# Runs of sixteen products, split down-weight loads and a finer end in a two-layer decoder trunk

## The chip, the cores and the metric

The kernel runs on one core of one Trainium2 chip. The core has a matrix engine (TensorE, PE in the profile, with its weight loads shown as PEld), a vector engine (VectorE, DVE), a scalar engine (ScalarE, ACT), GpSimd (POOL) and SyncE (SP), which here only sends DMA transfers. Each engine runs its own instruction list in order, and they wait for one another by semaphores. The metric is the device time in microseconds (us) of one execution. The kernel before takes 2140.93 us, the median of three runs (2140.59 to 2141.5).

## The reference

Two layers over 256 tokens of width 2048, all in float32. Each layer does, cut to what matters here:

```python
h = rmsnorm(x, attn_norm_g[l])
q, k, v, gate_b, gate_c, conv_in = split(h @ w_in[l])        # six parts of 1024 columns
attn = rmsnorm(diff_attention(rmsnorm(q), rmsnorm(k), v), subln_g[l])
conv = gate_b * short_conv(gate_c * conv_in, conv_w[l])      # causal, 3 taps
x = x + concat([attn, conv]) @ w_out[l]                      # 2048 x 2048
hm = rmsnorm(x, mlp_norm_g[l]) @ w_up[l]                     # 2048 x 8192
x = x + square(relu(hm)) @ w_down[l]                         # 8192 x 2048
```

The weights are read once; they are most of the traffic. The products are most of the work.

## The kernel before

**Numbers in two parts.** Every float32 operand of a product is split into a hi part and a lo part that the matrix engine can multiply, and a product is the sum of three: hi by hi, hi by lo, lo by hi. For weights ACT writes hi (a copy that rounds) and DVE writes lo (the original minus hi); in the program's names `whi` and `wlo`, and for the up projection `uhi` and `ulo`. Activations are kept as both parts side by side, so a matmul with the weight's hi part can take both parts of the activations at once. That is a wide matmul, 128x512; the one with the weight's lo part needs the hi part of the activations alone, and is narrow, 128x256.

**Weights.** `Weights.take()` hands out the next tile (hi, lo) of a list of jobs, and makes the tiles up to three ahead (`AHEAD`): it sends the DMA of a raw tile on SP's queue and puts the conversions on ACT and DVE. There are three buffers each for hi and lo (`wpool`), four for raw tiles. A conversion therefore waits for its raw tile to land and for PE to be done with the tile three before it; a load waits until the lo conversion of the tile four before it has read its buffer.

**Order of the work.** PE's list is exactly the order in which the program writes the matmuls (`manual_schedule`). ACT's, DVE's, SP's and POOL's lists are ordered by a scheduler that places each operation by its estimate of when it is ready and wanted, so that a change on PE moves operations on the others too. Small pieces of work (norms, attention, convolution) are kept as generators in `Background` and put between the matmuls by `work.tick()`.

**The mixer (q, k, v, conv).** `linear` does q, k, v and the output projection. `linear_t` (L392) does the three projections of the convolution branch, gate_C (`gc`), conv_in (`ci`) and gate_B (`gb`), with weights stationary: for each of four columns of 256 it goes through four weight tiles of 512x256, and for each tile through eight wide and then eight narrow matmuls. The gc and ci columns alternate, and beside them the attention of the second half of the heads runs in the background: scores (`sc`), the attention output's norm (`an`), its transposition (`atp`) and its split into `cat`. When the last attention buffers come free, the first four transfers of up weights (`uraw`, 1 MB each) are sent.

**The MLP, up.** 32 pairs of 2 x 128 hidden columns. A column's up projection (`up_part`, L941) takes two weight tiles of 1024 rows, and does eight wide and eight narrow matmuls with each; the result in the single bank tagged `av` (`upc`) is read by ACT as `ev` (L961), added by DVE to `h`, and for a pair squared and split into `f` (`square`, L964 to L984). From pair 2 on each column is followed by products of the pair two before (`LAG`) with rows of the down weights: a Strassen-like scheme that has seven products for eight, products 1, 2, 3 and 5 after the first column and 7, 6 and 4 after the second (`product`, L991). Its weights come from `quarters` (L833): `load_rows` (L826) sends one 1 MB transfer of two K tiles of 128 rows (`draw`), and from it come `b1h`, `b1l` (the first K tile's first half), `b2h`, `b2l` (the second K tile), the sums `t` and their halves `t13h`, `t13l`, `t24h`, `t24l` (L841 to L859). Two buffers hold the raw rows.

**The MLP, down.** The second half of the output columns is accumulated in blocks from the hidden values, which went out to DRAM as `hid`. At the end of a layer `onto` (L1049) adds an accumulator to the residual `xs`. In the last layer the very last block is done `by_token` (L1125): token tile 0 first over all of K, then tile 1. Then both tiles are added and `store` (L1112) sends them as two transfers on SP's queue.

Of the kernel before, what the change touches and what calls it, by code (L numbers as in the profile page):

```python
# [9 lines left out]
F32 = mybir.dt.float32  # L10
# [5 lines left out]
P = 128  # L16
# [3 lines left out]
NT = S // P  # L20
# [8 lines left out]
CH = 512  # L29
WC = 256  # L30
KG = 4
# [74 lines left out]
def trunk(ctx: ExitStack, tc: tile.TileContext, x, w_in, w_out, conv_w, q_norm_g, k_norm_g,  # L106
          lambda_q1, lambda_k1, lambda_q2, lambda_k2, subln_g, attn_norm_g, mlp_norm_g,
          w_up, w_down, rel_bias, selector, out):
    nc = tc.nc
# [8 lines left out]
    mm = ctx.enter_context(tc.tile_pool(name="mm", bufs=2, space=PSUM))  # L118
# [7 lines left out]
    def bank(name):  # L126
        return ps.tile([P, CH], F32, tag="bank", name=name)
# [264 lines left out]
    def linear_t(name, acts, weights):  # L392

        acc = mm.tile([P, 2, 2, S], F32, tag="mm2", name=name)
        nk = len(acts) * KG
        for k0 in range(0, nk, 4):
            hi, lo = weights.take()  # L400
            a = acts[k0 // KG]
            while not a.ready:
                work.tick()
            for part, wt in ((0, hi), (1, lo)):
                for k in range(k0, k0 + 4):
                    for f in range(2):
                        fs = slice(f * P, (f + 1) * P)
                        nc.tensor.matmul(  # L408
                            acc[:, f, 0] if part else acc[:, f], wt[:, k % 4, fs],
                            a.ap[:, 0, k % KG] if part else a.ap[:, :, k % KG],  # L410
                            start=(part == 0 and k == 0), stop=(part == 1 and k == nk - 1),
                            skip_group_check=True)
                    if k % 2:
                        work.tick()
        return acc
# [374 lines left out]
    def mlp(l, mnorm, last):  # L790
# [5 lines left out]
        with ExitStack() as scope:  # L796
# [28 lines left out]

            def load_rows(i, col, pool=dpool, tag="draw"):  # L826
                raw = pool.tile([P, 2, 2 * CH], F32, tag=tag, name=tag)
                nc.sync.dma_start(
                    raw, w_down[l][i * 2 * P:(i + 1) * 2 * P, col:col + 2 * CH].rearrange(
                        "(k p) c -> p k c", p=P))  # L830
                return raw

            def quarters(i, col=0):  # L833
# [104 lines left out]
                acc = ps.tile([P, CH], F32, tag="av", name="upc", bufs=1)  # L938
                return acc.rearrange("p (h s) -> p h s", h=2)

            def up_part(acc, kh):  # L941

                hi, lo = weights.take()
                for part, wt in ((0, hi), (1, lo)):
                    for k in range(8):
                        a = mT[kh * 2 + k // KG]
                        while not a.ready:
                            work.tick()  # L950
                        nc.tensor.matmul(  # L951
                            acc[:, 0] if part else acc, wt[:, k],
                            a.ap[:, 0, k % KG] if part else a.ap[:, :, k % KG],
                            start=(part == 0 and kh == 0 and k == 0),
                            stop=(part == 1 and kh == 1 and k == 7), skip_group_check=True)
                        if k % 4 == 3:
                            work.tick()

            def evict(acc, dst):
                ev = nat.tile([P, 2, S], F32, tag="wide", name="ev")  # L960
# [37 lines left out]
            for i in range(NP):  # L998
                j = i - LAG
                end = i == NP - 1  # L1000
                h = fpool.tile([P, 8, P], F32, tag="h", name="h", bufs=1)
                if i == 0:
                    two = mm.tile([P, 2, CH], F32, tag="mm2", name="up0")
                    two = [two[:, c].rearrange("p (h s) -> p h s", h=2) for c in range(2)]
                    for kh in range(2):
                        for c in range(2):
                            up_part(two[c], kh)
                    forms["plain"]()
                    for c in range(2):
                        evict(two[c], h[:, 2 * c:2 * c + 2])  # L1010
                    fs[0] = square(0, h)
                    forms["sums"]()
                    continue
                for c in range(2):
                    if i < LAG:
                        acc = bank("upw").rearrange("p (h s) -> p h s", h=2)
                    else:
                        acc = column_bank()
                    up_part(acc, 0)
                    up_part(acc, 1)  # L1020
                    evict(acc, h[:, 2 * c:2 * c + 2])
                    if c == 1:
                        fs[i] = square(i, h)
                    if j == 0 and c == 0:
                        for pair in ((1, 6), (2, 3)):
                            w2 = mm.tile([P, 2, CH], F32, tag="mm2", name=f"pr{l}{pair[0]}")
                            prods[pair[0]], prods[pair[1]] = w2[:, 0], w2[:, 1]
                        for n in (4, 5, 7):
                            prods[n] = bank(f"pr{l}{n}")
                    if j >= 0 and c == 0:  # L1030
                        b11, b21, b22 = weights.take()
                        t1, t3 = weights.take()
                        f = fs[j]
# [75 lines left out]
                    pair(2 * b + j, f, 4 * j)  # L1109
                return f  # L1110

            def store(n):  # L1112
                for t in range(NT):
                    nc.sync.dma_start(
                        out[0, t * P:(t + 1) * P, n * CH:(n + 1) * CH], xs[n][:, t])

            if last:
                store(0)
                store(1)


            accs = [mm.tile([P, NT, CH], F32, tag="mm2", name=f"dn{l}{n}") for n in range(2)]
            prods[2], prods[4] = accs[0][:, 0], accs[0][:, 1]
            prods[3], prods[8] = accs[1][:, 0], accs[1][:, 1]

            def by_token(f, n):

                parts = [weights.take() for _ in range(KG // 2)]
                for t in range(NT):
                    for k in range(KG):  # L1130
                        for m, (pa, pw) in enumerate(TERMS):
                            nc.tensor.matmul(
                                accs[n][:, t], f(k, pa, t), parts[k // 2][pw][:, k % 2],
                                start=False, stop=(k == KG - 1 and m == 2))
                        work.tick()

            def columns(f, n, start=False, stop=False):

                for kp in range(KG // 2):
                    hi, lo = weights.take()  # L1140
                    for k in (2 * kp, 2 * kp + 1):
                        for t in range(NT):
                            for m, (pa, pw) in enumerate(TERMS):
                                nc.tensor.matmul(  # L1144
                                    accs[n][:, t], f(k, pa, t), (hi, lo)[pw][:, k % 2],
                                    start=(start and k == 0 and m == 0),
                                    stop=(stop and k == KG - 1 and m == 2))
                        work.tick()
# [4 lines left out]
            for i in range(2 * BLK):  # L1153
# [6 lines left out]
                    continue  # L1160
                start, end = i == SEVEN[0], i == SEVEN[-1]
                if start:
                    for n in (1, 5, 6):
                        prods[n] = bank(f"pr{l}r{n}")
                    prods[7] = ps.tile([P, CH], F32, tag="av", name=f"pr{l}r7", bufs=1)
                b11, b21, b22 = weights.take()
                t1, t3 = weights.take()
# [14 lines left out]
            for b, n in order:  # L1182
                if n == 0 and b + 1 < NB2 - 1:
                    blocks[b + 1] = block(b + 1)
                units = lambda k, pa, t, f=blocks[b]: f[:, pa, 2 * k + t]
                if last and (b, n) == order[-1]:
                    by_token(units, n)
                else:
                    columns(units, n, stop=(b == NB2 - 2))
                if b == NB2 - 2:  # L1190
                    for t in range(NT):
                        onto(xs[2 + n][:, t], accs[n][:, t], xs[2 + n][:, t])
                    if last:
                        store(2 + n)
                    else:
                        work.start(norm.chunk(2 + n, (5, 2)[n]))
        return norm

# [45 lines left out]
```

## Time and profile before

| | |
|---|---|
| runs (three) | 2140.59 to 2141.5 us, median 2140.93 |
| profiled execution | 2141.7 us, its span 2139.9 us |
| TensorE clock granted | 1.00 |
| PE | 2129.0 us busy, 99%, 10,925 matmuls |
| DVE | 1699.2 us, 79% |
| ACT | 1316.2 us, 62% |
| chain that ended last | PE 97%, DVE 1%, ACT 1%, DMA 1% |
| largest groups of the chain | upc (L951) 31%, pr (L994) 13%, dn (L1076) 8%, o (L386) 8% |
| DMA | 476 MB, 222 GB/s over the span; 277 GB/s between 420 and 440 us |
| DVE between 420 and 440 us, and between 700 and 780 | 19.86 of 20, 70.56 of 80 |

The profile is of one execution. A row of a timeline has the start in us, the length, the engine, the line of the kernel, the operation, its result and operands, the shapes and a count where equal operations are joined; in square brackets stands the time in which the engine was idle before it and what ended that. A row of waits has the time in all, how many times and the longest. An "SPq" row is the sending of a DMA, not its transfer. The length of a matmul contains its filling and draining, which overlap with its neighbours, so that the time of a run of matmuls is read from start to start.

### The profile page before, as it was taken

What the parts mean: (1) busy time and instruction counts of PE and PEld (TensorE: products, weight loads), DVE (VectorE), ACT (ScalarE), POOL (GpSimd) and SP (SyncE); (2) the same over time, 40 slices, a digit from 0 to 9 for tenths busy, and PEclk for the clock granted to TensorE, in tenths of its full rate; (3) what the DMA queues carried; (4) which work ended last, traced back from release to release, by engine and by line L of the source; (5) the groups of instructions that cost most, each with busy time, mean ns of one, the idle gap of its engine ahead of it and who ended that gap; (6) DMA issues with size and microseconds to landing.
All of it is one profiled execution on the core that took longest, in us unless ns stands there. A gap on an engine that the chain in (4) does not pass through costs nothing.

```text
span 2139.9 us, 28980 instructions
## 1 busy us (share of the span) xinstructions
PE 2129.0 (99%) x10925; PEld 1817.0 (85%) x10925; DVE 1699.2 (79%) x2315; ACT 1316.2 (62%) x1776; POOL 164.3 (8%) x226
## 2 busy tenths in 40 slices
PE   9999999999999999999999999999999999999999
PEld 8888888888888888888888888888888888888887
DVE  6778655798888888798666776557888888888986
ACT  6666545666666666566566664446666666665653
POOL 3110200000000000001101101000000000000110
PEclk9999999999999999999999999999999999999999
DMA  7555866677777777788656558656777777777983
GB/s 273 178 162 168 257 187 187 195 243 229 234 233 229 229 236 225 240 301 302 219 177 178 167 162 262 188 167 213 240 235 221 241 228 226 237 226 258 317 307 121
DMA packets 296221, 475.98 MB, mean 222 GB/s; under 512 B 10804, under 2 KB 191622, under 8 KB 296081
## 3 DMA queue, kind: packets, MB, share of 16 engines
q1 hardware_dynamic: 267232, 406.88, 60.9%
q0 software_dynamic: 28800, 67.24, 9.4%
q8 instruction: 85, 1.39, 0.3%
q14 instruction: 56, 0.45, 0.1%
q10 hardware_dynamic: 48, 0.02, 0.0%
HBM read 440.52 MB, written 33.58 MB: 222 GB/s over the span
## 4 chain that ended last, share of the span: by engine, by line
PE 97%; DVE 1%; ACT 1%; DMA 1%; issue 0%; DVEq 0%; ACTq 0%
PE upc L951 31%; PE pr L994 13%; PE dn L1076 8%; PE o L386 8%; PE ci L408 4%; PE gb L408 4%; PE q L386 4%; PE k L386 4%; PE v L386 4%; PE gc L408 4%; PE dn L994 2%; PE dn L1144 2%; PE pr1r L994 1%; PE pr0r L994 1%; PE upw L951 1%; PE up L951 1%
## 5 line engine op out<-in xcount | busy, mean ns | idle before, releaser
L303 DVE TENSOR_TENSOR wlo<-raw,whi 128x1024 fp32r<-128x1024 f32 x274 | 341.7, 1248 | 221.1 <-ACT whi L302 219.6
L302 ACT ACTIVATE whi<-raw 128x1024 fp32r<-128x1024 f32 x274 | 290.4, 1060 | 306.8 <-PE o L386 73.6
L951 PE MATMUL upc<-nT,uhi 128*128 128x512 f32 x1920 | 477.6, 391 | 0.8 <-ACT ev L961 0.8
L818 ACT ACTIVATE uhi<-uraw 128x1024 fp32r<-128x1024 f32 x256 | 271.3, 1061 | 279.4 <-PE upc L951 259.8
L951 PEld LDWEIGHTS upc<-nT,uhi 128*128 128x128 f32 x1920 | 352.7, 188 | 69.4 <-ACT ev L961 1.2
L819 DVE TENSOR_TENSOR ulo<-uraw,uhi 128x1024 fp32r<-128x1024 f32 x256 | 312.5, 1221 | 108.8 <-ACT uhi L818 104.9
L951 PEld LDWEIGHTS upc<-nT,ulo 128*128 128x128 f32 x1920 | 261.9, 190 | 18.7
L951 PE MATMUL upc<-nT,ulo 128*128 128x256 f32 x1920 | 267.7, 282 | 0.0
L1076 PE MATMUL dn<-whi,fb 128*128 128x512 f32 x528 | 166.1, 389 | 0.0
L386 PE MATMUL o<-whi,cat 128*128 128x512 f32 x512 | 159.5, 390 | 0.0
L302 ACT ACTIVATE whi<-uraw 128x1024 fp32r<-128x1024 f32 x66 | 70.0, 1061 | 84.0 <-PE dn L1076 79.0
L1076 PEld LDWEIGHTS dn<-whi,fb 128*128 128x128 f32 x528 | 99.1, 188 | 20.6
L386 PEld LDWEIGHTS o<-whi,cat 128*128 128x128 f32 x512 | 96.1, 188 | 19.7
L842 DVE TENSOR_TENSOR t13l<-t,t13h 128x1024 fp32r<-128x1024 f32 x81 | 99.1, 1224 | 5.4 <-ACT t13h L841 3.3
L1076 PE MATMUL dn<-wlo,fb 128*128 128x512 f32 x264 | 102.7, 389 | 0.0
L841 ACT ACTIVATE b2h<-draw 128x1024 fp32r<-128x1024 f32 x81 | 85.6, 1057 | 25.3 <-PE pr L994 22.1
L842 DVE TENSOR_TENSOR b2l<-draw,b2h 128x1024 fp32r<-128x1024 f32 x81 | 98.7, 1218 | 2.3 <-ACT b2h L841 2.3
L842 DVE TENSOR_TENSOR t24l<-t,t24h 128x1024 fp32r<-128x1024 f32 x81 | 98.7, 1219 | 1.5 <-ACT t24h L841 0.3
L386 PE MATMUL o<-wlo,cat 128*128 128x512 f32 x256 | 99.6, 389 | 0.0
L855 DVE TENSOR_TENSOR t<-draw 128x1024 f32<-128x1024 f32 x81 | 98.7, 1218 | 0.5
L303 DVE TENSOR_TENSOR wlo<-uraw,whi 128x1024 fp32r<-128x1024 f32 x66 | 80.5, 1222 | 19.7 <-ACT whi L302 19.5
L994 PE MATMUL pr<-t13h,f 128*128 128x512 f32 x240 | 93.8, 391 | 0.0
(408 smaller groups left out, 4109.7 us busy)
## 6 DMA issues: line engine op xcount, KB each, us to landing
uraw<-in_w_up_dram SPq DMA_DIRECT2D x128, 1024.0 KB, 6.6
raw<-in_w_in_dram SPq DMA_DIRECT2D x191, 512.0 KB, 3.9
draw<-in_w_down_dram SPq DMA_DIRECT2D x85, 1024.0 KB, 5.5
uraw<-in_w_down_dram SPq DMA_DIRECT2D x33, 1024.0 KB, 5.8
raw<-in_w_out_dram SPq DMA_DIRECT2D x64, 512.0 KB, 3.7
hid0p<-f POOLq DMA_DIRECT2D x20, 512.0 KB, 6.9
raw<-in_w_down_dram SPq DMA_DIRECT2D x10, 1024.0 KB, 5.1
fb<-hid0p POOLq DMA_DIRECT2D x20, 512.0 KB, 6.9
```

The lines of the kernel that those rows point to most:

```text
L302: pair = (nc.scalar.activation(hi, raw, AF.Copy), nc.vector.tensor_sub(lo, raw, hi.bitcast(F32)))
L303: nc.vector.tensor_sub(lo, raw, hi.bitcast(F32)))
L386: nc.tensor.matmul(acc[:, t], a.ap[:, pa, k % KG, t * P:(t + 1) * P], (hi, lo)[pw][:, j], start=(k == 0 and n == 0), stop=(k == nk - 1 and ...
L408: nc.tensor.matmul(acc[:, f, 0] if part else acc[:, f], wt[:, k % 4, fs], a.ap[:, 0, k % KG] if part else a.ap[:, :, k % KG], start=(part ...
L818: pair = (nc.scalar.activation(hi, src, AF.Copy), nc.vector.tensor_sub(lo, src, hi.bitcast(F32)))
L819: nc.vector.tensor_sub(lo, src, hi.bitcast(F32)))
L841: keep(nc.scalar.activation(hi, src, AF.Copy))
L842: keep(nc.vector.tensor_sub(lo, src, hi.bitcast(F32)))
L855: keep(nc.vector.tensor_sub(t[:, 0:2], raw[:, :, 1], raw[:, 0]))
L951: nc.tensor.matmul(acc[:, 0] if part else acc, wt[:, k], a.ap[:, 0, k % KG] if part else a.ap[:, :, k % KG], start=(part == 0 and kh == 0 ...
L994: nc.tensor.matmul(prods[n], f[:, pa, a], b[pw], start=(start and m == 0), stop=(stop and m == 2))
L1076: nc.tensor.matmul(prods[p], f[:, pa, 2 * k + t], b[pw][:, n], start=(p in starts and k == 0 and m == 0), stop=(stop and k == 1 and m == 2))
```

## The change

- `linear_t` takes two tiles at a time and does sixteen wide matmuls, then sixteen narrow ones.
- `up_part` takes several halves; for pairs 1 to 31 a column's two tiles are done as sixteen wide and sixteen narrow ones. Pair 0 stays in eights.
- `load_rows` sends two transfers of 512 KB, one for each K tile.
- The banks of products 4, 5 and 7 are allocated in the order 5, 7, 4; in the last layer the second pair of accumulators of the down blocks are two single banks, and products 1 and 5 of the second stage share one two-bank tile.
- `store` sends one token tile, right after that tile is added; the last tile of the last block is added and sent in two halves of 256 columns, the first on SP's queue, the second on ACT's.

All matmuls, conversions and bytes are the same as before.

```diff
@@ linear_t
-        for k0 in range(0, nk, 4):
-            hi, lo = weights.take()
-            a = acts[k0 // KG]
-            while not a.ready:
-                work.tick()
-            for part, wt in ((0, hi), (1, lo)):
-                for k in range(k0, k0 + 4):
+        for k0 in range(0, nk, 8):
+            tiles = [weights.take() for _ in range(2)]
+            for part in range(2):
+                for k in range(k0, k0 + 8):
+                    a = acts[k // KG]
+                    while not a.ready:
+                        work.tick()
+                    wt = tiles[(k - k0) // 4][part]
                     for f in range(2):
...
@@ load_rows
-                nc.sync.dma_start(
-                    raw, w_down[l][i * 2 * P:(i + 1) * 2 * P, col:col + 2 * CH].rearrange(
-                        "(k p) c -> p k c", p=P))
+                for k in range(2):
+                    nc.sync.dma_start(
+                        raw[:, k], w_down[l][(i * 2 + k) * P:(i * 2 + k + 1) * P,
+                                             col:col + 2 * CH])
@@ up_part
-            def up_part(acc, kh):
+            def up_part(acc, *halves):
-                hi, lo = weights.take()
-                for part, wt in ((0, hi), (1, lo)):
-                    for k in range(8):
...
+                tiles = [weights.take() for _ in halves]
+                for part in range(2):
+                    for kh, wt in zip(halves, tiles):
+                        for k in range(8):
...
-                    up_part(acc, 0)
-                    up_part(acc, 1)
+                    up_part(acc, 0, 1)
-                        for n in (4, 5, 7):
+                        for n in (5, 7, 4):
                             prods[n] = bank(f"pr{l}{n}")
@@ accumulators of the down blocks
-            accs = [mm.tile([P, NT, CH], F32, tag="mm2", name=f"dn{l}{n}") for n in range(2)]
-            prods[2], prods[4] = accs[0][:, 0], accs[0][:, 1]
-            prods[3], prods[8] = accs[1][:, 0], accs[1][:, 1]
+            def two_banks(name):
+                both = mm.tile([P, NT, CH], F32, tag="mm2", name=name)
+                return [both[:, t] for t in range(NT)]
+            accs = [two_banks(f"dn{l}0"),
+                    [bank(f"dn{l}1{t}") for t in range(NT)] if last else two_banks(f"dn{l}1")]
+            (prods[2], prods[4]), (prods[3], prods[8]) = accs
...
-                    for n in (1, 5, 6):
-                        prods[n] = bank(f"pr{l}r{n}")
+                    prods[1], prods[5] = (two_banks(f"pr{l}r1") if last else
+                                          [bank(f"pr{l}r{n}") for n in (1, 5)])
+                    prods[6] = bank(f"pr{l}r6")
@@ end
-                        onto(xs[2 + n][:, t], accs[n][:, t], xs[2 + n][:, t])
-                    if last:
-                        store(2 + n)
-                    else:
+                        if last and (n, t) == (1, NT - 1):
+                            for half, queue in enumerate((nc.sync, nc.scalar)):
+                                at = slice(half * WC, (half + 1) * WC)
+                                onto(xs[3][:, t, at], accs[n][t][:, at], xs[3][:, t, at])
+                                store(3, t, half, queue)
+                            continue
+                        onto(xs[2 + n][:, t], accs[n][t], xs[2 + n][:, t])
+                        if last:
+                            store(2 + n, t)
+                    if not last:
                         work.start(norm.chunk(2 + n, (5, 2)[n]))
```

More of the change, by code (lines that the diff above doesn't have):

```diff
@@ L939, in column_bank @@
                 return acc.rearrange("p (h s) -> p h s", h=2)
-            def up_part(acc, kh):
-                hi, lo = weights.take()
-                for part, wt in ((0, hi), (1, lo)):
-                    for k in range(8):
[L948 to L957, printed above, removed]
+            def up_part(acc, *halves):
[3 more added lines that the diff above has]
+                        for k in range(8):
+                            a = mT[kh * 2 + k // KG]
+                            while not a.ready:
+                                work.tick()
+                            nc.tensor.matmul(
+                                acc[:, 0] if part else acc, wt[part][:, k],
+                                a.ap[:, 0, k % KG] if part else a.ap[:, :, k % KG],
+                                start=(part == 0 and kh == 0 and k == 0),
+                                stop=(part == 1 and kh == 1 and k == 7), skip_group_check=True)
+                            if k % 4 == 3:
+                                work.tick()
             def evict(acc, dst):
@@ L1110, in block, with store @@
                 return f
[L1112 to L1115, printed above, removed]
+            def store(n, t, half=None, queue=nc.sync):
+                at = slice(0, CH) if half is None else slice(half * WC, (half + 1) * WC)
+                queue.dma_start(
+                    out[0, t * P:(t + 1) * P, n * CH + at.start:n * CH + at.stop], xs[n][:, t, at])
             if last:
-                store(0)
-                store(1)
-            accs = [mm.tile([P, NT, CH], F32, tag="mm2", name=f"dn{l}{n}") for n in range(2)]
-            prods[2], prods[4] = accs[0][:, 0], accs[0][:, 1]
-            prods[3], prods[8] = accs[1][:, 0], accs[1][:, 1]
+                for n in range(2):
+                    for t in range(NT):
+                        store(n, t)
+            def two_banks(name):
[4 more added lines that the diff above has]
+            (prods[2], prods[4]), (prods[3], prods[8]) = accs
             def by_token(f, n):
@@ L1132, in by_token @@
                             nc.tensor.matmul(
-                                accs[n][:, t], f(k, pa, t), parts[k // 2][pw][:, k % 2],
+                                accs[n][t], f(k, pa, t), parts[k // 2][pw][:, k % 2],
                                 start=False, stop=(k == KG - 1 and m == 2))
@@ L1144, in columns @@
                                 nc.tensor.matmul(
-                                    accs[n][:, t], f(k, pa, t), (hi, lo)[pw][:, k % 2],
+                                    accs[n][t], f(k, pa, t), (hi, lo)[pw][:, k % 2],
                                     start=(start and k == 0 and m == 0),
```

## The prediction

> **What bounds the kernel now.** I read the page's busy times first, then the waits of TensorE (PE), and only then the timelines at those places.
>
> ```profile
> PE 2129.0 (99%) x10925; PEld 1817.0 (85%) x10925; DVE 1699.2 (79%) x2315; ACT 1316.2 (62%) x1776; POOL 164.3 (8%) x226
> ...
> L951 PE MATMUL upc<-nT,uhi 128*128 128x512 f32 x1920 | 477.6, 391 | 0.8 <-ACT ev L961 0.8
> ```
>
> ```profile
> PE pr L994 <- DVE f L984: 3.2, 2, 1.7
> PE sc L604 <- DVE cat L682: 1.2, 2, 0.6
> PE upc L951 <- ACT ev L961: 0.8, 1, 0.8
> ```
>
> PE is busy for 99% of the span, so the time is that of its matmuls, in an order written by hand. Only three things can move it: what one matmul takes, the few microseconds in which PE waits (these rows: in total, times, longest), and what lies behind its last matmul. The change keeps every matmul; it alters the order of widths, who is late at the waits, and the end. The sum is made against the profiled execution, 2141.7 us (span 2139.9 and 1.8 around it), which stands 0.8 above the median of 2140.93.
>
> **Runs of one width.** A column of the up projection and its neighbours:
>
> ```profile
> 702.04 1.98 PE L951 MATMUL upc<-nT,uhi 128*128 128x512 f32 x8
> 703.85 1.12 PE L951 MATMUL upc<-nT,ulo 128*128 128x256 f32 x8
> 704.80 2.00 PE L951 MATMUL upc<-nT,uhi 128*128 128x512 f32 x8
> 706.64 1.11 PE L951 MATMUL upc<-nT,ulo 128*128 128x256 f32 x8
> ```
>
> From start to start, eight wide matmuls take 1.81 us behind products as wide as themselves and 1.84 behind a narrow run. So a change from narrow to wide costs 0.03, less some 0.01 that the narrow run may get back and that rounding hides: I take 0.02, with ends 0.01 and 0.03. With sixteen and sixteen one such change goes in each of 124 up columns (31 pairs, 2 columns, 2 layers; pair 0 stays) and two in each of 24 columns of linear_t (three projections, 4 columns, 2 layers): 172 x 0.02 = **-3.4 us**, ends -1.7 and -5.2. A sentence apart: the Trainium skill ("TensorE: Matmul & The Clock Gate", Back-to-back issue gap) gives the spacing as a function of the moving width alone, by which the order of widths is worth nothing and the sum below would be 3.4 us higher; the 0.03 between 1.81 and 1.84 speaks against it, and it is a rival below.
>
> **What sixteen in a row needs earlier.** In linear_t the second tile's hi half is now wanted straight behind the first, one narrow run (0.95) earlier, and the lo buffer of the first tile is freed 1.8 us later. Each pair of tiles also sends two loads. With three buffers of each half a tile is elsewhere converted well ahead of its use; not where the norm's release sends the first up weights (four transfers of 1 MB) among the loads of the last ci column:
>
> ```profile
> 231.16 0.37 SPq L343 DMA_DIRECT2D raw<-in_w_in_dram  x1
> 232.60 3.17 SPq L811 DMA_DIRECT2D uraw<-in_w_up_dram  x3
> 235.87 4.55 SPq L343 DMA_DIRECT2D raw<-in_w_in_dram  x1
> ```
>
> ```profile
> 247.27 1.06 ACT L302 ACTIVATE whi<-raw 128x1024 fp32r<-128x1024 f32 x1 [2.00 <-DMA raw<-in_w_in_dram]
> 251.34 1.06 ACT L302 ACTIVATE whi<-raw 128x1024 fp32r<-128x1024 f32 x1 [3.01 <-DMA raw<-in_w_in_dram]
> ```
>
> ```profile
> 244.37 2.00 PE L408 MATMUL ci<-nT,whi 128*128 128x512 f32 x8
> 246.21 1.11 PE L408 MATMUL ci<-nT,wlo 128*128 128x256 f32 x8
> 247.16 2.00 PE L408 MATMUL ci<-nT,whi 128*128 128x512 f32 x8
> ```
>
> Before, the second ci tile was issued at 231.16, ahead of the up weights; the third came behind three of them (235.87) and could be converted only at 247.27, the fourth at 251.34. In the changed program's SP queue it is the second tile that stands behind three up weights (its issue waits for a lo conversion that now comes after the norm's an), and the third behind all four. Transfers of one queue land in turn, so the second tile gets the place of the row at 247.27: hi ready at 248.33, wanted at 244.37 + 1.81 = 246.2, late by 2.1. The third gets 251.34, ready at 252.40, wanted 3.7 after the second began, at 252.05: late by 0.35 more. The squares in front of the norm no longer queue behind a whi of 1.06 on ACT, so I let the up weights go some 0.7 earlier: 1.4 + 0.35 + 0.1 for PE's restart = 1.9. Layer 1:
>
> ```profile
> 1310.44 1.06 ACT L302 ACTIVATE whi<-raw 128x1024 fp32r<-128x1024 f32 x1 [2.53 <-DMA raw<-in_w_in_dram]
> ```
>
> ```profile
> 1307.02 2.00 PE L408 MATMUL ci<-nT,whi 128*128 128x512 f32 x8
> ...
> 1315.56 2.11 PE L408 MATMUL ci<-nT,whi 128*128 128x512 f32 x8
> ```
>
> Likewise 1311.50 against 1308.8, less 0.7, with 0.45 behind it, is 2.4; some 0.3 of waiting at 1315.56 is in the time already. Together **+4.0 us**, ends +1.0 (up weights 2 us earlier) and +5.4 (no earlier).
>
> Scores wait for cat (1.2 us in the second rows above):
>
> ```profile
> 163.17 0.74 DVE L682 SCALAR_TENSOR_TENSOR cat<-atp,s_gain,cat 128x512 fp32r<-128x512 f32 x1
> 163.83 1.21 DVE L303 TENSOR_TENSOR wlo<-raw,whi 128x1024 fp32r<-128x1024 f32 x1
> ```
>
> The lo conversion that stood behind cat now stands ahead of it, on a DVE that must wait for the freed lo buffer first; cat ends some 0.3 later in each layer: **+0.6**, ends -1.2 (the wait vanishes) and +2.4 (the whole 1.2 in both).
>
> **Start of the MLP.** The long waits for f go back to late down weights:
>
> ```profile
> 445.71 0.37 SPq L811 DMA_DIRECT2D uraw<-in_w_up_dram  x1
> 446.31 0.40 SPq L828 DMA_DIRECT2D draw<-in_w_down_dram  x1
> ```
>
> ```profile
> 456.44 0.63 ACT L841 ACTIVATE b1h<-draw 128x512 fp32r<-128x512 f32 x1 [4.21 <-DMA draw<-in_w_down_dram]
> ...
> 1520.61 0.63 ACT L841 ACTIVATE b1h<-draw 128x512 fp32r<-128x512 f32 x1 [5.47 <-DMA draw<-in_w_down_dram]
> ```
>
> That draw was issued right behind an uraw and held ACT for 4.21 and 5.47 us, and with it the squares and f. In the changed order it goes ahead of that uraw, in two halves, so b1h needs only the first. The waits for f and ev, 3.2 + 0.8 and about 0.8 for restarts and rounding, go: **-4.8**. What is late next, with the first down rows of the product phase:
>
> ```profile
> 417.96 1.22 DVE L819 TENSOR_TENSOR ulo<-uraw,uhi 128x1024 fp32r<-128x1024 f32 x1
> 419.10 1.22 DVE L842 TENSOR_TENSOR t13l<-t,t13h 128x1024 fp32r<-128x1024 f32 x1
> ```
>
> ```profile
> 428.68 0.63 ACT L841 ACTIVATE b1h<-draw 128x512 fp32r<-128x512 f32 x1 [0.58 <-DMA draw<-in_w_down_dram]
> 429.22 1.05 ACT L841 ACTIVATE b2h<-draw 128x1024 fp32r<-128x1024 f32 x1
> ```
>
> ```profile
> 421.29 0.39 PE L994 MATMUL pr<-t13l,f 128*128 128x512 f32 x1
> ...
> 429.37 1.98 PE L951 MATMUL upc<-nT,uhi 128*128 128x512 f32 x8
> ```
>
> A second ulo now stands ahead of t13l: 419.10 + 1.14 + 1.22 = 421.5 against 421.3, 0.2 late. And b1h, an uhi and b2h stand ahead of the eviction ev (0.6) that frees the single column bank for the column at 429.37; before, ev came first. The second half lands about when the whole did (428.68): b2h ends at 429.7, ev at 430.2, 0.6 late after the 0.2. Layer 1:
>
> ```profile
> 1493.41 0.63 ACT L841 ACTIVATE b1h<-draw 128x512 fp32r<-128x512 f32 x1 [2.40 <-DMA draw<-in_w_down_dram]
> ```
>
> ```profile
> 1492.28 1.98 PE L951 MATMUL upc<-nT,uhi 128*128 128x512 f32 x8
> ```
>
> There b2h starts at 1493.4 at best and ev ends at 1495.0 for 1492.28, 2.5 late with the 0.2. New waits 1.0 + 2.7 = **+3.7** with restarts, ends 0 and +6. Net -1.1.
>
> **Other edits.** The added DMA issues (0.37 each on SP, which mostly waits) delay the uraw behind them by as much; uraws are converted far behind their landing, so nothing; without that cover 0.4 per pair would reach PE. Products in the order 5, 7, 4 and the other accumulator banks sit behind PE's matmuls: nothing. The end:
>
> ```profile
> 2135.02 0.39 PE L1132 MATMUL dn<-whi,fb 128*128 128x512 f32 x1
> ```
>
> ```profile
> 2135.45 1.41 DVE L1049 SCALAR_TENSOR_TENSOR x<-dn,rowf,x 128x512 f32<-128x512 f32 x2 [4.03 <-PE dn L1132]
> ```
>
> ```profile
> DMA to landing us min/median/max: 2.1/4.6/9.2
> ```
>
> by_token finishes token tile 0 first, but one accumulator over both banks kept DVE waiting 4.03 us for the whole, then two updates took 1.41. With single banks tile 0 is updated under tile 1's matmuls, and tile 1 follows in halves of some 0.4: the last store is sent 2 x 0.70 - 2 x 0.38 = 0.65 earlier and lands in about 2.1 as before. **-0.65**, ends -0.3 (a half costs nearly a whole) and -0.9.
>
> **Sum.** 2141.7 - 3.4 + 4.0 + 0.6 - 1.1 - 0.65 = 2141.15 for a profiled execution, less the 0.8 above: **2140.4 us** in the median. I forecast no change that can be told: about 0.2%, 4.3 us, is what a measurement of this kernel can tell from none (2136.6 to 2145.2).
>
> **Rivals.** *The new waits don't come* (faster). The up weights and the first down halves go out earlier than I read from the order. Without new waits at the MLP's start 3.7 less, 2136.7; with the ci tiles at their early end 3.0 less as well, 2133.7; without any new wait about 2132. For it: sixteen matmuls of cover on either side, and draws that go ahead of the uraws. Against it: in both layers the SP queue put one load in its place behind three transfers, and the rows at 247.27 and 1310.44 show what that place costs.
>
> *The split rows land late* (slower). In the changed order b1h and b2h stand ahead of an eviction in every pair, and there is one column bank.
>
> ```profile
> raw<-in_w_in_dram SPq DMA_DIRECT2D x191, 512.0 KB, 3.9
> draw<-in_w_down_dram SPq DMA_DIRECT2D x85, 1024.0 KB, 5.5
> ```
>
> Landing is 3.9 for a half's size against 5.5 for a whole: two in turn would be 7.8, 2.3 more. It decides once b2h ends behind its column's last matmul in the steady pairs and not in the first alone; at 0.13 us in each of 62 pairs it costs 8: 2148. A sentence apart: the Trainium skill ("DMA: Bandwidth & Descriptors", Measured) asks for transfers of 1 MiB or more, and its fit of 2.0 us plus bytes at 436 GB/s gives halves 3.2 each against 4.4; if they are paid in series that is 2.0 more per row. Against it: the conversions at 251.34 and 252.73 follow two loads of 512 KB only 1.39 apart, so loads in one queue overlap all but their bytes.
>
> ```profile
> 252.73 1.06 ACT L302 ACTIVATE whi<-raw 128x1024 fp32r<-128x1024 f32 x1 [0.33 <-DMA raw<-in_w_in_dram]
> ```
>
> *The runs bring nothing*: 1.84 is what a restart behind a narrow run costs wherever it stands, and the sum is 2143.8.
>
> **Chances.** My forecast 0.40, its own range 2137 to 2144 (its terms each within half of their ends). New waits absent or halved 0.37, from 2132 to 2136.6. Split rows late 0.19, from 2145.2 up. Runs that bring nothing 0.04. So faster 0.37, within 0.2% 0.44, slower 0.19. The range for 8 in 10 reaches to 2133 (a tenth lies below, all waits gone) and to 2147 (a tenth above).
>
> **What would show it.** Right: wide matmuls in the up columns 1.81 per eight throughout; PE waits of 1 to 2.5 us for whi in the last ci column of both layers, for ev early in both MLPs, and none for f; two half updates of some 0.4 behind PE's last matmul in place of 1.41. Wrong: any wait for ev or b1l in the steady product phase; no wait in ci; eight wide ones still 1.84 behind another wide run; waits at places I haven't named, since two loads and two conversions at a time move every small operation of the attention beside linear_t by up to 1.2 us.

## The result, and the profile after

The changed kernel takes 2147.49 us (median of six runs, 2145.76 to 2150.48) against 2141.30 (six runs, 2140.59 to 2141.8): 1.0027 of the time before, with a 95% interval of 1.0017 to 1.0038. It is slower, by 6.2 us, just outside the predicted range and on the side that was given a chance of 0.19. A second measurement beside other kernels gave 1.0028 (1.0018 to 1.0038), with one execution at 2154.1. Its runs also spread more: 4.7 and 9.3 us against 1.2 and 3.6.

The profiled execution took 2146.97 us, its span is 2145.2. The waits of PE in it (in total, times, longest):

```profile
PE sc L605 <- DVE cat L683: 4.8, 2, 2.4
PE ci L409 <- ACT whi L302: 2.6, 2, 1.6
PE upc L954 <- ACT ev L964: 1.9, 2, 1.2
PE warm L160 <- DVE mhalf L152: 1.1, 1, 1.1
PE pr L997 <- DVE t13l L844: 0.8, 2, 0.4
PE q L386 <- DVE wlo L303: 0.3, 1, 0.3
```

The waits for f are gone; the one for cat is four times what it was, and those for ci, ev and t13l come where they were foreseen. The second finding is in the clock. Behind the first wait for cat, PE's timeline reads:

```profile
162.54 1.09 PE L409 MATMUL gc<-nT,whi 128*128 128x512 f32 x4
163.47 0.22 PE L605 MATMUL sc<-kT,qT 128*128 128x128 f32 x1
166.07 0.55 PE L605 MATMUL sc<-kT,qT 128*128 128x256 f32 x1 [2.38 <-DVE cat L683]
166.42 0.63 PE L605 MATMUL sc<-kL,qT 128*128 128x128 f32 x2
166.85 0.63 PE L605 MATMUL sc<-kT,qT 128*128 128x128 f32 x2
167.27 0.63 PE L605 MATMUL sc<-kL,qT 128*128 128x128 f32 x2
167.70 5.13 PE L409 MATMUL gc<-nT,whi 128*128 128x512 f32 x12
172.67 2.08 PE L409 MATMUL gc<-nT,wlo 128*128 128x256 f32 x16
```

and the windows over the same stretch (busy time and count of each engine, then PEclk, the granted TensorE clock, the DMA share and GB/s):

```profile
164.00:166.00 2.00, 0.00 (x0) 0.00 (x0) 2.00 (x4) 0.50 (x1) 0.00 (x0) 0.91 0.84 261
166.00:168.00 2.00, 1.93 (x8) 1.96 (x9) 0.96 (x4) 0.00 (x0) 0.00 (x0) 0.50 0.81 235
168.00:170.00 2.00, 2.00 (x6) 1.52 (x6) 0.99 (x7) 0.30 (x1) 0.00 (x0) 0.50 0.08 28
170.00:172.00 2.00, 2.00 (x7) 1.52 (x6) 0.00 (x0) 2.00 (x8) 0.00 (x0) 0.50 0.00 0
172.00:174.00 2.00, 2.00 (x15) 1.85 (x14) 0.12 (x1) 1.57 (x4) 0.00 (x0) 0.89 0.00 0
174.00:180.00 6.00, 6.00 (x38) 5.35 (x37) 5.51 (x10) 2.73 (x3) 1.30 (x1) 1.00 0.53 161
```

The clock is granted at 0.50 from 165.6, while PE still idles, until 172.5. Twelve wide matmuls take 4.97 us from start to start, 0.41 each against 0.23. PE is "busy" all through it, so the page's 99% shows nothing. The same wait in layer 1 (2.39 us) had no such stretch behind it in this execution.

Putting PE's position in the two programs side by side gives the account of the 5.3 us in the spans. Each term is the change of the distance between the same matmul before and after:

| part | layer 0 | layer 1 | worked out before |
|---|---|---|---|
| start, wait for a wlo at 18 us | +0.3 | | not named |
| scores waiting for cat, and the clock behind it | +4.7 | +1.7 | +0.6 for the two together |
| last ci column | +2.3 | +1.1 | +4.0 for the two together |
| start of the MLP, with gb's runs | +0.1 | -1.7 | -1.1, the runs apart |
| runs: gc and ci, steady up columns | -1.3 | -1.3 | -3.4 in all |
| end | | -0.65 | -0.65 |

The runs: a column of the steady up phase is 708.50 to 714.03, 5.53 us, where the rows of before had 702.04 to 707.60, 5.56. A single pair of rows is too coarse for this. In layer 0 the up column that starts at 471.35 before starts 7.03 us later after the change, and the one 52 columns on, at 885.61, starts 6.00 later: 0.02 us gained in each.

```profile
708.50 3.79 PE L954 MATMUL upc<-nT,uhi 128*128 128x512 f32 x16
712.12 2.08 PE L954 MATMUL upc<-nT,ulo 128*128 128x256 f32 x16
714.03 0.40 PE L997 MATMUL pr<-b1h,f 128*128 128x512 f32 x1
```

**Why cat was late.** The rows of DVE and ACT ahead of the wait at 163.47. After:

```profile
163.38 0.75 DVE L761 SCALAR_TENSOR_TENSOR v<-v,rowf,v 128x512 fp32r<-128x512 f32 x1 [0.43 <-ACT v L760]
164.05 1.21 DVE L303 TENSOR_TENSOR wlo<-raw,whi 128x1024 fp32r<-128x1024 f32 x1
165.18 1.40 DVE L683 SCALAR_TENSOR_TENSOR cat<-atp,s_gain,cat 128x512 fp32r<-128x512 f32 x2
```

```profile
160.63 2.01 ACT L302 ACTIVATE whi<-raw 128x1024 fp32r<-128x1024 f32 x2
162.66 0.69 ACT L760 ACTIVATE v<-v,rowf 128x512 fp32r<-128x512 f32 x1
163.25 1.26 ACT L682 ACTIVATE cat<-atp,s_gain 128x512 fp32r<-128x512 f32 x2
```

and ACT, and v on DVE, before (the prediction shows the cat and the wlo behind it, at 163.17 and 163.83):

```profile
160.27 1.06 ACT L302 ACTIVATE whi<-raw 128x1024 fp32r<-128x1024 f32 x1
161.36 0.69 ACT L759 ACTIVATE v<-v,rowf 128x512 fp32r<-128x512 f32 x1
162.51 0.74 DVE L760 SCALAR_TENSOR_TENSOR v<-v,rowf,v 128x512 fp32r<-128x512 f32 x1
```

Two whi in a row stand ahead of v's evacuation on ACT, v's on DVE waits for that, and the extra wlo stands between v and cat: cat starts at 165.18 where it started at 163.17. Of these 2.01 us, 0.34 are from the start. v on DVE comes 0.53 later still, by the second whi (162.51 to 163.38, less the 0.34), and the wlo adds 1.14. Scores need the bank that cat empties.

### The profile page after: what moved, and what is told of

The parts are those of the page before. It is cut to its first block, busy times and chain, and to the rows that moved or that the text cites. A ratio compares the mean times of both kernels' runs of the same rounds, so it can differ in the third digit from the quotient of the medians.

```text
span 2145.2 us, 29286 instructions
## 1 busy us (share of the span) xinstructions
PE 2129.6 (99%) x10925; PEld 1820.2 (85%) x10925; DVE 1688.9 (79%) x2316; ACT 1345.8 (63%) x1776; POOL 164.5 (8%) x226
## 5 line engine op out<-in xcount | busy, mean ns | idle before, releaser
L303 DVE TENSOR_TENSOR wlo<-raw,whi 128x1024 fp32r<-128x1024 f32 x274 | 332.5, 1222 | 206.5 <-ACT whi L302 164.7
L954 PE MATMUL upc<-nT,uhi 128*128 128x512 f32 x1920 | 455.1, 389 | 1.9 <-ACT ev L964 1.9
L954 PEld LDWEIGHTS upc<-nT,uhi 128*128 128x128 f32 x1920 | 360.1, 188 | 77.5 <-ACT ev L964 2.8
L954 PEld LDWEIGHTS upc<-nT,ulo 128*128 128x128 f32 x1920 | 246.2, 191 | 9.4
L954 PE MATMUL upc<-nT,ulo 128*128 128x256 f32 x1920 | 249.1, 283 | 0.0
L964 ACT ACTIVATE ev<-upc 128x512 f32<-128x512 f32 x120 | 71.8, 599 | 48.5 <-PE upc L954 48.5
L843 ACT ACTIVATE t24h<-t 128x1024 fp32r<-128x1024 f32 x81 | 86.1, 1063 | 21.7 <-PE pr L997 15.9
```

What stands on the lines that cost most here:

```text
L303: nc.vector.tensor_sub(lo, raw, hi.bitcast(F32)))
L843: keep(nc.scalar.activation(hi, src, AF.Copy))
L954: nc.tensor.matmul(acc[:, 0] if part else acc, wt[part][:, k], a.ap[:, 0, k % KG] if part else a.ap[:, :, k % KG], start=(part == 0 and kh ...
```

## The experiments

All ratios are against the kernel before on the same chip, measured beside it; there it had medians of 2142.32, 2142.19 and 2141.76 us. A ratio is taken over all executions and differs from the quotient of the medians by up to 0.0004.

| kernel | median us | ratio (95% interval) |
|---|---|---|
| linear_t in eights, all else changed | 2138.36 | 0.9986 (0.9977 to 0.9995) |
| only linear_t in sixteens | 2150.20 | 1.0036 (1.0023 to 1.0048) |
| only the up columns in sixteens | 2141.83 | 1.0001 (0.9992 to 1.0010) |
| only the down rows split | 2140.66 | 0.9996 (0.9987 to 1.0005) |
| changed, with PE kept at work through the wait for cat | 2144.88 | 1.0012 (1.0003 to 1.0021) |
| changed, first gc and last ci column in eights | 2141.91 | 0.9999 (0.9990 to 1.0008) |
| that, and the start of the MLP as before | 2138.25 | 0.9978 (0.9970 to 0.9987) |
| only the first gc column in sixteens | 2146.65 | 1.0023 (1.0015 to 1.0032) |
| linear_t in eights, start of the MLP as before | 2135.01 | 0.9970 (0.9959 to 0.9980) |
| that, and gb in sixteens | 2135.12 | 0.9973 (0.9963 to 0.9983) |
| changed, once more | 2147.04 | 1.0028 (1.0018 to 1.0038) |

### Which part of the change costs the time

Theory A was that linear_t does it; rival B, that the split loads or the up runs do. The first kernel takes back linear_t alone:

```diff
-        for k0 in range(0, nk, 8):
-            tiles = [weights.take() for _ in range(2)]
+        for k0 in range(0, nk, 4):
+            hi, lo = weights.take()
```

> The changed kernel with linear_t back in eights; up runs, split loads and the new end stay. Theory A (the sixteens in linear_t cost the time: an extra whi on ACT and an extra wlo on DVE ahead of cat make the scores wait 2.4 us in each layer, the clock falls behind that wait, and the last ci column waits): the scores wait about 1.2 us in all as before, no wait for whi in ci, clock 1.000, and 2137.5 us (2136 to 2139). Rival B (the split loads or the up runs cost it): still 2145 or more.

Its median is 4.0 us below that of before. In its profiled execution PE waits for cat 1.2 us and not at all in ci, and the clock is 1.000; the waits for ev (2.3) and t13l (0.8) at the MLP's start stay. One of its eleven executions took 2143.58, with a mean clock of 0.998; what PE waited for in it is not known.

The second has the new linear_t in the kernel before, and nothing else:

```diff
-        for k0 in range(0, nk, 4):
+        for k0 in range(0, nk, 8):
```

> The kernel before with only linear_t in sixteens. Theory A: waits for cat 4.8 us in place of 1.2 and 2.6 in ci, 0.9 gained by the runs: 2146 if the clock never falls, some 3 more for each execution's fall, so 2146 to 2151 with more spread than the kernel before. Rival B: 2140 to 2142.

It is 7.9 us slower. Its waits of PE:

```profile
PE sc L605 <- DVE cat L683: 4.8, 2, 2.4
PE pr L995 <- DVE f L985: 3.3, 2, 1.7
PE ci L409 <- ACT whi L302: 2.8, 2, 1.7
PE warm L160 <- DVE mhalf L152: 1.1, 1, 1.1
```

In its profiled execution the clock fell behind both waits for cat (mean 0.998). So linear_t alone costs what the changed kernel lost and 2 us more, and A stands.

The third and the fourth do the other two parts alone:

```diff
-                    up_part(acc, 0)
-                    up_part(acc, 1)
+                    up_part(acc, 0, 1)
```

> The kernel before with only the up columns in sixteens. The steady part of the changed kernel gained 1.1 us per layer over 430 us, so 2.3 in all; what the start of the MLP makes of it is open: with its 4.8 us of waits kept 2139.0, with new waits for t13l and ev as in the changed kernel and those for f gone 2138, with both 2142. Rival B would have it at 2143 or more.

```diff
-                nc.sync.dma_start(raw, w_down[l][i * 2 * P:(i + 1) * 2 * P, col:col + 2 * CH]...)
+                for k in range(2):
+                    nc.sync.dma_start(raw[:, k], w_down[l][(i * 2 + k) * P:(i * 2 + k + 1) * P, ...])
```

> The kernel before with only the down rows loaded in two halves. If the halves cure the late b1h (4.2 and 5.5 us of ACT waiting), the waits for f go: 2137. If the order of SP's queue, not the size, made it late, the waits stay: 2141.3. Rival B: 2143 or more, from rows landing later.

Neither can be told from the kernel before. In both the start of the MLP trades one wait for another. Up runs alone: f's 3.2 us are gone, and ev waits 4.0 and t13l 2.0; the time is that of the third case of its expectation, by larger new waits and not by old ones kept. Split rows alone: f falls from 3.2 to 0.9 and ev rises from 0.8 to 3.0. The split does not cure the start, and it costs nothing in the steady phase; rival B falls. The longest executions of the up runs alone, 2145.5 and 2146.2 us, had a mean clock of 0.998; in the profiled one PE waited 2.4 us for ev and the clock stayed.

### Which column of linear_t, and what the wait does to the clock

```diff
-                acc = linear_t(f"gc{l}{q}", hT, weights)
+                acc = linear_t(f"gc{l}{q}", hT, weights, 1 if q else 2)   # tiles at once; others 1
```

> The kernel before with only the first gc column of each layer in sixteens. Theory A: the scores wait 4.8 us in place of 1.2, no wait in ci, and the clock falls in some executions: 2144.9 without a fall, 2147.5 with one, so 2144.5 to 2150. If the wait needs the other columns too: 2141 to 2142.

One column of twelve in each layer makes 4.5 us of the loss: its PE waits 4.8 us for cat and none in ci. In the profiled execution the clock stayed at 1.00 behind both 2.4 us waits, and twelve wide matmuls took their ordinary time:

```profile
166.45 0.36 PE L605 MATMUL sc<-kT,qT 128*128 128x256 f32 x1 [2.40 <-DVE cat L683]
...
167.33 2.90 PE L409 MATMUL gc<-nT,whi 128*128 128x512 f32 x12
```

Its eleven executions run from 2145.37, with a mean clock of 1.000, to 2150.86, with 0.997. To see whether the idling itself is the cause, the next kernel keeps cat as late as it is and gives PE work meanwhile: the first score matmul of head 4 twenty times over, each writing the same.

```diff
             sc = [bank(f"sc{h}_{m}") for m in range(2)]
+            if h == 4:
+                for _ in range(20):
+                    nc.tensor.matmul(sc[0][:, :P], qT[:, 0, i, :P], kT[:, 0, i, :P],
+                                     start=True, stop=False, skip_group_check=True)
```

> The changed kernel, with the first score matmul of head 4 written twenty times over in each layer, ahead of the one that waits for cat: PE has some 2 us of work in place of idling, cat comes no earlier. Theory A (idling for 2.4 us is what makes the granted clock fall): the wait of 2.4 us shrinks to some 0.3, no matmul runs at half rate behind it, clock 1.000 in every execution, 2144.2 us against about 2147.5 for the changed kernel, and the spread narrower. Rival C (the clock falls for another reason, such as the load before it): matmuls of 427 ns behind the scores as before, 2147 or more.

```profile
163.15 2.35 PE L603 MATMUL sc<-kT,qT 128*128 128x128 f32 x20
165.33 0.27 PE L609 MATMUL sc<-kT,qT 128*128 128x128 f32 x1
165.75 0.35 PE L609 MATMUL sc<-kT,qT 128*128 128x256 f32 x1 [0.15 <-DVE cat L687]
...
166.64 2.93 PE L409 MATMUL gc<-nT,whi 128*128 128x512 f32 x12
```

Cat comes no earlier, the scores go on when they did, and the twelve matmuls behind them take 2.9 us and not 5.1. The median is 2144.88 against some 2147.3, about as expected. The clock wasn't 1.000 throughout, as the expectation had it: in the profiled execution it fell at another place, behind a wait for ev of 2.1 us at the MLP's start:

```profile
435.38 5.53 PE L958 MATMUL upc<-nT,uhi 128*128 128x512 f32 x16 [2.11 <-ACT ev L968]
```

Sixteen wide matmuls in 5.4 us from start to start, where 3.6 is ordinary. In the profiled executions of this study PE waited eleven times for 2.0 us or more, and six of these waits have a half-rate stretch behind them; none has that was shorter. So idling comes before every fall, but the length of the wait alone does not decide.

**What decides is in the traces.** In all thirteen profiles the granted clock changes only at points that lie whole multiples of 3.413 us apart: in the changed kernel at 5.21, 165.63 and 172.46 us, which is 47 and 2 of them. It stays at 0.50 for one such interval in five cases (3.41 us) and for two in one (6.83). Cut at these points, the profiles have 8,123 intervals at full clock. In 19 of them PE idled for 1.94 us or more (six at the waits, thirteen behind PE's last matmul), and behind each of these the clock was 0.50 in the next interval; in none of the others did PE idle for more than 1.90, and the clock stayed. The first two rows are of the changed kernel, around the waits for cat in layer 0 and layer 1, the third of the kernel with only the first gc column in sixteens; idle is the length less PE's busy time, the first two figures (to 0.01, by rounding):

```profile
162.22:165.63 3.41, 1.47 (x10) 1.07 (x8) 2.98 (x4) 2.26 (x4) 0.00 (x0) 1.00 0.61 193
1230.59:1234.00 3.41, 1.52 (x10) 1.12 (x8) 2.97 (x4) 2.31 (x4) 0.00 (x0) 1.00 0.61 192
162.24:165.65 3.41, 1.81 (x13) 1.41 (x10) 2.97 (x4) 2.61 (x4) 0.00 (x0) 1.00 0.59 192
```

Of the wait in layer 0, 1.94 us lie in the interval, and the next one ran at 0.50. Of the wait in layer 1, 1.90 lie in it and 0.49 in the next, and of the third 1.61 and 0.79: the clock stayed. A wait of 2.4 us therefore costs its length alone or more, by where it falls among the intervals, and they lie differently in each execution. The two intervals at half rate are the one case in which PE still idled (0.44 us) in the first of them. This is read from the traces afterwards: no kernel here moves a wait against the intervals. Rival C falls, by the 2.4 us that the filled wait gains and by these rows.

### Putting the two columns back, and the start of the MLP

```diff
-                acc = linear_t(f"gc{l}{q}", hT, weights)
+                acc = linear_t(f"gc{l}{q}", hT, weights, 2 if q else 1)
...
-                acc = linear_t(f"ci{l}{q}", hT, weights)
+                acc = linear_t(f"ci{l}{q}", hT, weights, 1 if q == 3 else 2)
```

> The changed kernel with only the first gc column and the last ci column of each layer in eights; the other eighteen columns of linear_t, the up runs, the split and the end stay. Theory A (the cost sits in these two columns alone): scores wait 1.2 us in all, ci none, clock 1.000, and some 0.7 us faster than with all of linear_t in eights (18 columns, two changes of width each, 0.02): 2137.6 us. If the cost lies in the sixteens wherever they stand: 2140 or more.

This missed by 4.3 us. The scores are cured (1.2), but ci still waits 2.2 us, now for its second and third tile: the gc column ahead of it is in sixteens, so the loads still go out in pairs and the second ci tile's load still stands behind three up weights. Eights where the tiles are used don't help where the load was sent late. And ev waits 3.1, one of these waits being 2.0 us with the clock falling behind it.

Next, on top of that, the start of the MLP:

```diff
+                if i in (2,) and col == 0:      # load_rows: pair 2 in one transfer
...
+                    if i <= 2:                  # up columns of pairs 1 and 2 in eights
+                        up_part(acc, 0)
+                        up_part(acc, 1)
+                    else:
+                        up_part(acc, 0, 1)
```

> As the one with the mixed linear_t, and at the start of the MLP pairs 1 and 2 in eights and the down rows of pair 2 in one transfer, so that the eviction ev again stands ahead of b1h and b2h on ACT, and one ulo less ahead of t13l. If these two orders make the waits of 0.8 (t13l) and 1.9 to 2.3 (ev) at the MLP's start, they go: 3 us less, 2134.6. If the late rows make them whatever the order, the time stays at 2137.6.

It is 3.7 us faster than without it, where 3.0 was expected; its time of 2138.25 misses the 2134.6 of the expectation all the same, since that started from the 2137.6 that had just been missed. All waits of the MLP are gone:

```profile
PE ci L409 <- ACT whi L302: 3.0, 3, 1.1
PE sc L605 <- DVE cat L683: 1.2, 2, 0.6
PE warm L160 <- DVE mhalf L152: 1.1, 1, 1.1
```

So at the start it is the order (ev behind b2h on ACT, a second ulo ahead of t13l on DVE) that makes the waits: ACT has ev at 430.03 ahead of b1h at 431.81, where the kernel without this edit has b1h at 429.16, b2h at 430.65 and ev at 431.60. The edit changes the loads and the columns together, so how much each of the two does for it is not shown. With ci's waits left, linear_t goes back to eights altogether:

```diff
-    def linear_t(name, acts, weights, at_once=2):
+    def linear_t(name, acts, weights, at_once=1):      # and no column asks for more
```

> The up runs (from pair 3 on), the split rows (from pair 3 on) and the new end, with linear_t all in eights. The waits at the start of the MLP are cured by their order (shown with the mixed linear_t) and linear_t has none but cat's 1.2: against the one with linear_t in eights (0.9986 of before) 3 us less, so 2135.5 where before stands at 2142, ratio 0.997. If the start's order depended on the shift that linear_t gave it, ev or f waits come back: 2138.

2135.01 us, 0.9970 of before (0.9959 to 0.9980), 0.5 from what was expected, and faster than both kernels. Its PE waits least of all, and its clock is 1.000 in every execution:

```profile
PE sc L605 <- DVE cat L683: 1.2, 2, 0.6
PE warm L160 <- DVE mhalf L152: 1.1, 1, 1.1
PE pr L1002 <- DVE f L992: 0.4, 1, 0.4
PE ci L409 <- ACT whi L302: 0.4, 1, 0.4
PE q L386 <- DVE wlo L303: 0.3, 1, 0.3
```

The last variant adds sixteens for gb alone:

```diff
-                acc = linear_t(f"gb{l}{q}", hT, weights)
+                acc = linear_t(f"gb{l}{q}", hT, weights, 2)
```

> As the one before it, with the four gb columns of each layer in sixteens, which have no attention beside them and no up weights ahead of their loads: 16 changes of width less, 0.3 us, so 2135.2 and not to be told from it. If sixteens wait wherever they stand (the rival): a wait for whi in gb and 2137 or more.

2135.12, not to be told from it, with no wait in gb: sixteens are harmless there, and their 0.3 us too small to see.

The changed kernel as it is, once more:

> The changed kernel once more, beside the others on one chip and with more executions: 1.0027 of before, with a spread of several us; executions whose mean granted clock is below 1 are the longer ones, some 3 us for each 0.0015 of the clock (6 us at half rate in 2145).

The nine executions sort as expected: those with a mean clock of 0.999 took 2144.8 to 2146.6, those with 0.998 2146.8 to 2148.2, and the one with 0.996 2154.1. In its profiled execution the half-rate stretch was 3.41 us long, not 6.83, and the span 2143.0 in place of 2145.2.

## Why the prediction was wrong

**The step that failed is the term "scores wait for cat", +0.6.** It was put as a lo conversion that moves ahead of cat and makes it 0.3 later in each layer, with an end of +2.4 for the whole wait again in both layers. It measured 3.6 us more waiting (4.8 for 1.2). The mechanism was right and its size was off. The wlo alone makes cat 1.14 later in each layer, which the prediction's own rows had (cat at 163.17 and the wlo of 1.21 behind it); the 0.3 has no working. The second whi on ACT, which holds v's evacuation and so v on DVE ahead of that wlo, makes another 0.53 and was not counted at all. The 3.0 us that were missing here would still have left the time inside the forecast's range.

**What was missing altogether is the clock.** The forecast priced a wait at its length. In layer 0 the wait of 2.4 us cost some 3 us more than that (+4.7 in the table against +1.7 in layer 1, where the clock stayed), and the 3.0 of cat and these 3 are nearly the whole miss: the terms of the forecast come to -0.55, and the spans differ by +5.3. The Trainium skill ("TensorE: Matmul & The Clock Gate", What's actually happening) describes such a gate, with a free-running window of about 3.4 us, after which an idle array is throttled to half. The trace agrees with the half (0.50 granted, 427 ns per wide matmul), with the window's length (changes of the clock only at multiples of 3.413 us) and with its not being tied to the kernel: whether the fall comes depends on how much of a wait lies in one window. It does not agree that the array must idle for a whole window. The Trainium skill (the same page, HAM oscillation) warns of idle gaps above 3.4 us; here 1.94 us within one window were enough and 1.90 were not, and the measurement decides. So that the profiled execution lost 3 us in one layer and none in the other is chance; other executions lost less or more (2144.8 to 2154.1).

**The other terms.** *Runs, -3.4:* about -2.6 measured outside gb and -0.3 in it (44.70 us before and 44.53 after in layer 0); the 0.02 for each change of width is what the steady columns show. *Last ci column, +4.0:* +3.4; right in place and cause, about right in layer 0, and half in layer 1, where the wait was 0.99 us for some 2. The load of the second tile did go out behind three up weights: its conversion came at 251.54 (ACT waited 3.45 us for the DMA) and PE waited 1.57 us, where 1.4 was worked out for layer 0.

```profile
251.54 1.06 ACT L302 ACTIVATE whi<-raw 128x1024 fp32r<-128x1024 f32 x1 [3.45 <-DMA raw<-in_w_in_dram]
```

```profile
252.65 2.14 PE L409 MATMUL ci<-nT,whi 128*128 128x512 f32 x8 [1.57 <-ACT whi L302]
```

*Start of the MLP, -1.1:* -1.6 with gb's runs in it, so -1.3 without; the waits for f went as foreseen, and those for t13l (0.4 in each layer for 0.2) and ev (1.2 and 0.7 for 0.6 and 2.5) came. That the net comes out so near is partly luck: the new waits are 2.7 and not 3.7, and the old ones that went were 4.0, without the 0.8 added for restarts. *End, -0.65:* from PE's last matmul to the end of the span 3.87 us in place of 4.52, so -0.65. Tile 0 was added at 2138.65 under tile 1's matmuls, and the two halves followed:

```profile
2141.37 0.88 DVE L1051 SCALAR_TENSOR_TENSOR x<-dn,rowf,x 128x256 f32<-128x256 f32 x2 [1.97 <-PE dn L1141]
```

**The rivals.** *The new waits don't come:* all came. *The split rows land late:* the slower side came true, but not this way; there is no wait for b1 or ev in the steady product phase, and split alone is 0.9996. The halves land in 5.0 us (median of the 170 in the changed kernel's profile), where the whole rows took 5.5. *The runs bring nothing:* they brought the 0.02 per change that was taken. The text named, as what would make it wrong, small attention operations beside linear_t moving by up to 1.2 us; that is where it went, with two of them in a row.

## What to carry to other kernels

When a change makes a helper take two tiles at a time, count what it puts ahead of each small operation on every in-order engine along that operation's chain, not on the last one alone: here one conversion more on ACT and one on DVE made one cat 1.7 us later. Look for such places beside the loop that is changed, and leave the first column, or the columns whose loads go out beside a burst, in the old form; check where the load was sent, not where the tile is used. And price a TensorE wait of 2 us or more above its length, since the clock may fall behind it; in this case matmuls that write nothing new, put into the wait, kept it up.

## What the runs showed of the hardware

The granted TensorE clock fell to 0.50 behind six of eleven idle stretches of 2.0 to 2.4 us, for 3.41 or 6.83 us, in some executions and not in others of the same program. It changed only at points 3.413 us apart, and fell exactly where PE had idled for 1.94 us or more between two of them (1.90 was not enough). That turned a fixed wait into a spread of several us between runs (2144.8 to 2154.1 for the changed kernel, 2134.6 to 2136.4 for the one without such waits). Work that PE repeats to no purpose, 20 matmuls of 0.11 us, kept the clock at full rate at the place where it was put.
